# Turning a residual from features to tokens by DVE squares and DMAs in place of the tensor engine

## The chip, the core and the metric

One Trainium2 chip; the kernel runs on one of its cores. The metric is the device time of one execution in microseconds (us). The kernel before takes 696.79 us, the median of three runs (696.49 to 696.87).

Engines: PE (TensorE: matmuls, and transposes by a matmul with the identity), DVE (VectorE), ACT (ScalarE), POOL (GpSimd) and SP (SyncE, which issues most DMAs). Each works through its own queue in order; semaphores tie them together.

## The reference

One layer of a decoder on 512 tokens with 1024 features, in float32:

```python
h = rms_norm(x, mix_norm)
z = h @ w_in                       # u_A | v_A | c_q | c_kv | k_rope | gate_A | gate_B
y_a = chunked_spatial_gating(gelu(u_a), gelu(v_a), ...)   # 4 chunks of 128 tokens, 8 groups
y_b = latent_attention(c_q, c_kv, k_rope, ...)            # 8 heads, causal
x = x + (sigmoid(g_a) * y_a + sigmoid(g_b) * y_b) @ w_out
up = causal_depthwise_conv(rms_norm(x, ffn_norm) @ w_up)  # 2 x 2816 channels, width 3
gate, val = split(up)
x = x + (silu(gate) * val) @ w_down
out = rms_norm(x, final_norm)
```

The x after the mixers is the residual of this text. It is needed twice: by features, as the input of the up-projection, and by tokens, where the result of the down-projection is added to it.

## The kernel before

Tiles have 128 partitions. Matrices of float32 are split into a rounded part (H or h, made by ACT) and a rest (L or l, made by DVE), and each product is three matmuls (`mm3`, L79 to L82): H by H, H by L, L by H. A weight tile of 128x1024 is loaded by SP (`wtile`, names wr_...), and `wsplit` makes wh_... on ACT (L70) and wl_... on DVE (L71). Three buffers each serve raw tiles, wh and wl.

Stages: small projections and attention inputs, attention and gates by head, the output projection (`pout0` to `pout7`, L563 to L580), which leaves the residual by features in x1 (eight tiles x1[j] of 128 features by 512 tokens) and its normed halves in h0f to h7f; the up-projection; the down-projection.

The up-projection is a loop over n = 0 to 21 (L653). Each n makes two up groups, `up(2n)` and `up(2n+1)`, of 24 matmuls on PE into a bank `pup`, and a convolution on ACT and DVE for each (z is its scaled input, y its sum); `a_sides` builds from the results aT the left operands of the down-projection (a1h, a1l, s1, s4). In passes n = 4 to 11 `x1_turn` (L645) turns the residual from features to tokens: four transposes on PE (L649) into a bank pt and one ACT copy back into x1's own place (L650). In passes 12 to 17 `fill` (L604) names the load of the weight tiles r1_0, r1_2, ... r1_10 (R[0] to R[5]), which have memory of their own.

The down-projection is seven products, m1, m5, m6, m4, m3, m7, m2, each over the six weight tiles in R, in that order on PE. After R[g] is split, POOL adds the next weights onto it by an accumulating DMA, or SP loads it anew. `plus` and `done` (L726, L729) add products to the residual by tokens, `finish` (L736) norms and stores it.

A scheduler sets the order on each engine at build time: by the order of the source, by what its model of time holds ready, and by when a buffer's memory is free. A DMA of SP also waits for one of eight lanes (DMAHW0 to DMAHW7), so for an earlier DMA on the same lane.

Of the kernel before, what the change touches and what calls it, by code (L numbers as in the profile page):

```python
# [7 lines left out]
F32 = mybir.dt.float32  # L8
# [15 lines left out]
NF = DFF // P  # L24
# [18 lines left out]
def block_kernel(ctx, tc, xT, pos, w_s, w_v, w_g, w_q, w_kv, w_o, w_u, w_d,  # L43
                 ws_t, bs, vg, vb, par, cst, fnl, out):
    nc = tc.nc
    V, A, T, G, SY = nc.vector, nc.scalar, nc.tensor, nc.gpsimd, nc.sync
# [61 lines left out]
    ident = cstt[:, CI:CI + P]  # L108
# [66 lines left out]
    cqL = [mx.tile([P, S], F32R, name=f"cqL{i}") for i in range(2)]  # L175
    ckH = mx.tile([P, S], F32R, name="ckH")
    ckL = mx.tile([P, S], F32R, name="ckL")
    vA2 = [hp.tile([P, 2 * D], F32, tag=f"d{t}", name=f"vA{t}") for t in range(2)]
    vA = [vA2[t // 2][:, (t % 2) * D:(t % 2 + 1) * D] for t in range(NT)]

    with tc.tile_pool(name="st", bufs=2) as st:

# [22 lines left out]
        for j in range(KC):  # L205
# [7 lines left out]
            lo = half * S  # L213
# [3 lines left out]
            for f in range(4):  # L217
                c = slice(lo + f * P, lo + (f + 1) * P)
# [321 lines left out]
    with tc.tile_pool(name="mg", bufs=2) as mg:  # L540
        for h in range(H):
            zb = zbs[h] if h in zbs else gate("b", 2 * H + h)
            pm = bank(f"pm{h}")
            c = slice(h * P, (h + 1) * P)
            for n in range(NT):
                T.matmul(pm[:, n * P:(n + 1) * P], lhsT=vA[n][:, c], rhs=wst[:, h], start=True, stop=True)
            t2 = mg.tile([P, S], F32, tag="t2", name=f"t2{h}")
            V.tensor_tensor(out=t2.rearrange("p (n t) -> p n t", n=NT),
                            in0=pm.rearrange("p (n t) -> p n t", n=NT),
                            in1=bsb[:, h:h + 1].to_broadcast([P, NT, P]), op=ALU.add)  # L550
            V.tensor_tensor(out=t2, in0=uT[h], in1=t2, op=ALU.mult)
            zz = mg.tile([P, S], F32, tag="zz", name=f"zz{h}")
            V.tensor_tensor(out=zz, in0=zb, in1=yB[h], op=ALU.mult)
            V.tensor_tensor(out=zz, in0=zz, in1=t2, op=ALU.add)
            mH.append(uy.tile([P, S], F32R, tag=f"u{h}", name=f"mH{h}"))
            mL.append(uy.tile([P, S], F32R, tag=f"y{h}", name=f"mL{h}"))
            split(mH[h], mL[h], zz)


        x1t = [hp.tile([P, NT, NT, P], F32, tag=f"d{t}", name=f"x1_{t}") for t in range(2)]  # L560
        x1 = [x1t[j // NT][:, j % NT].rearrange("p t c -> p (t c)") for j in range(KC)]
        acc2 = hp.tile([P, S], F32, name="acc2")
        for j in range(KC):  # L563
            SY.dma_start(x1[j], xT[j])
            raw = wtile(w_o[j], f"o{j}")
            wh, wl = wsplit(raw, f"o{j}")
            po = bank(f"pout{j}")
            for h in range(H):
                c = slice(h * P, (h + 1) * P)
                mm3(po, wh[:, c], wl[:, c], mH[h], mL[h], h == 0, h == H - 1)  # L570
            V.tensor_tensor(out=x1[j], in0=po, in1=x1[j], op=ALU.add)
            htiles(j, "f")
            g_ = part[:, PFF + j:PFF + j + 1]
            A.mul(hH[j], x1[j], g_)
            V.scalar_tensor_tensor(out=hL[j], in0=x1[j], scalar=g_, in1=hH[j].bitcast(F32),
                                   op0=ALU.mult, op1=ALU.subtract)
# [18 lines left out]
    NS = len(steps)  # L595
    B11, B12, B21, B22 = (w_d[k, f] for k in range(2) for f in range(2))

    R = [fp.tile([P, (hi - lo) * S], F32, name=f"r1_{lo}") for lo, hi in steps]

    def cols(g):  # L600
        lo, hi = steps[g]
        return slice(lo * S, hi * S)

    def fill(q, g, add=True):  # L604
        if add:
            G.dma_start(R[g], q[:, cols(g)], accum_op=ALU.add)  # L606
        else:
            SY.dma_start(R[g], q[:, cols(g)])

# [32 lines left out]
                               op0=ALU.mult, op1=ALU.add)  # L642
        return y

    def x1_turn(t, hf):  # L645

        pt = bank(f"pt{t}{hf}")
        for q in range(NT):
            T.transpose(pt[:, q * P:(q + 1) * P], x1t[hf][:, q, t, :], ident)  # L649
        A.copy(x1t[hf][:, :, t, :], pt.rearrange("p (q c) -> p q c", q=NT))  # L650

    with tc.tile_pool(name="f2", bufs=2) as f2:
        for n in range(NF):  # L653
# [12 lines left out]
            if n % 4 == 3 or n == NF - 1:
                a_sides(n // 4 * 2, n // 2 + 1)
            if 4 <= n < 12:
                x1_turn((n - 4) // 2, n % 2)
            if 12 <= n < 12 + NS:  # L670
                fill(B11, n - 12, False)

# [43 lines left out]

    def res(t, f):

        return x1t[f][:, :, t, :]

    def b3(t):
        return t.rearrange("p (q c) -> p q c", q=NT)

    def plus(t, f, t_):  # L726
        V.tensor_tensor(out=res(t, f), in0=res(t, f), in1=b3(t_), op=ALU.add)

    def done(t, f, p_, op=ALU.add):  # L729
        V.tensor_tensor(out=res(t, f), in0=res(t, f), in1=b3(p_), op=op)  # L730
        j_ = dp.tile([P, S], F32, tag="j", name=f"j{t}{f}", bufs=2)
        A.activation(out=b3(j_), in_=res(t, f), func=AF.Square, accum_out=ms[:, t, f:f + 1])
        if f:
            V.tensor_tensor(out=res(t, f), in0=res(t, f), in1=b3(gfb[:, S:]), op=ALU.mult)

    def finish(t):  # L736

        V.tensor_scalar(out=ms[:, t, 2:3], in0=ms[:, t, 0:1], scalar1=ms[:, t, 1:2], scalar2=1.0 / D,
                        op0=ALU.add, op1=ALU.mult)
        V.tensor_scalar(out=ms[:, t, 2:3], in0=ms[:, t, 2:3], scalar1=EPS, scalar2=None, op0=ALU.add)  # L740
        G.tensor_tensor(out=ms[:, t, 3:4], in0=ms[:, t, 2:3], in1=mhalf[:, 0:1], op=ALU.pow)
        r_ = ms[:, t, 3:4]
        V.scalar_tensor_tensor(out=res(t, 0), in0=res(t, 0), scalar=r_, in1=b3(gfb[:, :S]),
                               op0=ALU.mult, op1=ALU.mult)
        A.mul(res(t, 1), res(t, 1), r_)
        SY.dma_start(out[t, :, :S], res(t, 0))
        A.dma_start(out[t, :, S:], res(t, 1))
# [143 lines left out]
```

## Time and profile before

| | |
|---|---|
| median of three runs | 696.79 us |
| the profiled execution | 697.01 us, its span 695.3 us |
| busy: PE, DVE, ACT, POOL | 684.6, 522.6, 353.9, 36.0 us |
| chain of waits | PE 96%, DVE 1%, issue 1% |
| mean granted clock of TensorE | 0.996 |
| DMA | 78.67 MB, mean 113 GB/s |

Busy times say how much each engine works; the chain says whose work decides the end. Here both name PE, which is almost never idle. The span runs from the first to the last instruction; the rest of an execution's time lies around it.

### The profile page before, as it was taken

What the parts mean: (1) busy time and instruction counts of PE and PEld (TensorE: products, weight loads), DVE (VectorE), ACT (ScalarE), POOL (GpSimd) and SP (SyncE); (2) the same over time, 40 slices, a digit from 0 to 9 for tenths busy, and PEclk for the clock granted to TensorE, in tenths of its full rate; (3) what the DMA queues carried; (4) which work ended last, traced back from release to release, by engine and by line L of the source; (5) the groups of instructions that cost most, each with busy time, mean ns of one, the idle gap of its engine ahead of it and who ended that gap; (6) DMA issues with size and microseconds to landing.
All of it is one profiled execution on the core that took longest, in us unless ns stands there. A gap on an engine that the chain in (4) does not pass through costs nothing.

```text
span 695.3 us, 8489 instructions
## 1 busy us (share of the span) xinstructions
PE 684.6 (98%) x3183; PEld 569.4 (82%) x3183; DVE 522.6 (75%) x859; ACT 353.9 (51%) x519; POOL 36.0 (5%) x42
## 2 busy tenths in 40 slices
PE   9999999999999999999999999999999999999994
PEld 6888888888888888888888888888888888888883
DVE  7966699877768678855577868778677789579884
ACT  6465556775765552343354344444344335565672
POOL 0000110000000000000100000000000002330201
PEclk9999999999999999999999999999999999999998
DMA  8424522131120112353542222223322236997824
GB/s 269 153 78 139 186 84 83 61 115 31 61 88 34 62 61 91 109 177 107 180 170 90 92 91 90 92 90 99 114 91 91 91 91 118 197 187 202 159 76 122
DMA packets 28026, 78.67 MB, mean 113 GB/s; under 512 B 3024, under 2 KB 7632, under 8 KB 27984
## 3 DMA queue, kind: packets, MB, share of 16 engines
q1 hardware_dynamic: 21408, 62.92, 27.4%
q0 software_dynamic: 3456, 11.54, 9.3%
q10 hardware_dynamic: 3120, 3.67, 1.7%
q8 instruction: 25, 0.41, 0.2%
q14 instruction: 17, 0.14, 0.1%
HBM read 76.02 MB, written 2.10 MB: 112 GB/s over the span
## 4 chain that ended last, share of the span: by engine, by line
PE 96%; DVE 1%; issue 1%; POOL 0%; ACT 0%; POOLq 0%
PE pup L80 12%; PE pup L82 12%; PE pup L81 11%; PE m L82 4%; PE m L81 4%; PE m L80 4%; PE pout L81 2%; PE pv L80 2%; PE pout L80 2%; PE pza L81 2%; PE pza L80 2%; PE pzb L80 2%; PE pzb L82 2%; PE pzu L81 2%; PE pzb L81 2%; PE pv L82 2%
## 5 line engine op out<-in xcount | busy, mean ns | idle before, releaser
L70 ACT CAST wh_u<-wr_u 128x1024 fp32r<-128x1024 f32 x44 | 46.3, 1051 | 84.4 <-issue 49.6
L71 DVE TENSOR_TENSOR wl_u<-wr_u,wh_u 128x1024 fp32r<-128x1024 f32 x44 | 53.9, 1224 | 9.9 <-ACT wh_u L70 9.6
L635 DVE TENSOR_TENSOR z<-pup,r 128x512 f32<-128x512 f32 x44 | 30.3, 690 | 40.3 <-PE pup L82 40.3
L82 PE MATMUL m<-wh_m,al_m 128*128 128x512 f32 x132 | 51.5, 390 | 0.6 <-DVE al_m L77 0.6
L80 PE MATMUL m<-wh_m,ah_m 128*128 128x512 f32 x132 | 51.4, 389 | 0.0
L81 PE MATMUL m<-wl_m,ah_m 128*128 128x512 f32 x132 | 51.4, 389 | 0.0
L70 ACT CAST wh_g<-wr_g 128x1024 fp32r<-128x1024 f32 x24 | 25.2, 1049 | 49.4 <-issue 30.6
L71 DVE TENSOR_TENSOR wl_m<-r,wh_m 128x1024 fp32r<-128x1024 f32 (+1 forms) x36 | 40.7, 1131 | 6.3 <-ACT wh_m L70 6.3
L70 ACT CAST wh_m<-r 128x1024 fp32r<-128x1024 f32 (+1 forms) x36 | 35.3, 980 | 19.6 <-PE m L82 19.1
L637 ACT ACTIVATE y<-z,part 128x512 f32<-128x512 f32 x44 | 35.7, 814 | 2.6 <-DVE z L635 2.4
L663 ACT ACTIVATE y<-y 128x512 f32<-128x512 f32 x22 | 13.9, 633 | 45.0 <-DVE y L641 45.0
L606 POOL DMA_DIRECT2D r<-in_w_d_dram x24 | 21.4, 890 | 287.0 <-DVE wl_m L71 270.7
L71 DVE TENSOR_TENSOR wl_g<-wr_g,wh_g 128x1024 fp32r<-128x1024 f32 x24 | 29.4, 1223 | 7.2 <-ACT wh_g L70 7.1
L641 DVE SCALAR_TENSOR_TENSOR y<-z,part,y 128x512 f32<-128x512 f32 x44 | 33.0, 751 | 1.4
L639 DVE SCALAR_TENSOR_TENSOR y<-z,part,y 128x512 f32<-128x512 f32 x44 | 32.8, 747 | 0.7 <-ACT y L637 0.7
L82 PEld LDWEIGHTS m<-wh_m,al_m 128*128 128x128 f32 x132 | 24.8, 188 | 6.1 <-DVE al_m L77 1.0
L81 PEld LDWEIGHTS m<-wl_m,ah_m 128*128 128x128 f32 x132 | 24.8, 188 | 5.2
L80 PEld LDWEIGHTS m<-wh_m,ah_m 128*128 128x128 f32 x132 | 24.8, 188 | 5.2
L81 PE MATMUL pout<-mL,wh_o 128*128 128x512 f32 x64 | 25.3, 395 | 0.0
L80 PE MATMUL pout<-mH,wh_o 128*128 128x512 f32 x64 | 25.0, 394 | 0.0
L82 PE MATMUL pout<-mH,wl_o 128*128 128x512 f32 x64 | 24.9, 389 | 0.0
L77 DVE TENSOR_TENSOR al_m<-aT,ah_m 128x1024 fp32r<-128x1024 f32 (+1 forms) x12 | 13.6, 1134 | 11.9 <-ACT ah_m L76 11.9
(565 smaller groups left out, 2004.0 us busy)
## 6 DMA issues: line engine op xcount, KB each, us to landing
wr_u<-in_w_u_dram SPq DMA_DIRECT2D x44, 512.0 KB, 3.3
wr_g<-in_w_g_dram SPq DMA_DIRECT2D x24, 512.0 KB, 3.4
r<-in_w_d_dram POOLq DMA_DIRECT2D x20, 512.0 KB, 7.2
r<-in_w_d_dram SPq DMA_DIRECT2D x10, 512.0 KB, 6.1
x<-in_xT_dram SPq DMA_DIRECT2D x16, 256.0 KB, 4.5
wr_v<-in_w_v_dram SPq DMA_DIRECT2D x8, 512.0 KB, 4.1
wr_o<-in_w_o_dram SPq DMA_DIRECT2D x8, 512.0 KB, 3.2
wr_m<-in_w_d_dram SPq DMA_DIRECT2D x5, 512.0 KB, 3.5
```

The source lines that it names most:

```text
L70: A.copy(th[:, lo:hi], raw[:, lo:hi])
L71: V.tensor_tensor(out=tl[:, lo:hi], in0=raw[:, lo:hi], in1=th[:, lo:hi].bitcast(F32), op=ALU.subtract)
L77: V.tensor_tensor(out=tl, in0=src, in1=th.bitcast(F32), op=ALU.subtract)
L80: T.matmul(o, lhsT=wh, rhs=xh, start=start, stop=False)
L81: T.matmul(o, lhsT=wh, rhs=xl, start=False, stop=False)
L82: T.matmul(o, lhsT=wl, rhs=xh, start=False, stop=stop)
L606: G.dma_start(R[g], q[:, cols(g)], accum_op=ALU.add)
L635: V.tensor_tensor(out=z[:, 2:], in0=pz, in1=r2, op=ALU.mult)
L637: A.activation(out=y, in_=z[:, 2:], func=AF.Identity, scale=part[:, w + 2:w + 3], bias=part[:, PCB + f:PCB + f + 1])
L639: V.scalar_tensor_tensor(out=y, in0=z[:, 1:S + 1], scalar=part[:, w + 1:w + 2], in1=y, op0=ALU.mult, op1=ALU.add)
L641: V.scalar_tensor_tensor(out=y, in0=z[:, 0:S], scalar=part[:, w:w + 1], in1=y, op0=ALU.mult, op1=ALU.add)
L663: A.activation(out=yg, in_=yg, func=AF.Silu)
```

## The change

x1 becomes one tile of memory "d" (and so does vA, which holds it earlier). DVE transposes each x1[j] in squares of 32 by 32 into a new tile xq (`squares`, two calls in each of the passes n = 0 to 3). 128 DMAs on SP then move the squares to their places in a tile xt, by tokens (`x1_turn`, eight DMAs of 32x4x32 elements in each of the passes n = 4 to 19). xt has the tag "d" too, so it takes x1's memory. xq0 to xq3 share the memory of r1_0 to r1_6, and `fill` is called in the last six passes, in the order 4, 5, 0, 1, 2, 3. The functions of the down-projection index xt by rows of 512 in place of pieces of 128.

```diff
--- before.py
+++ after.py
@@ -175,8 +175,8 @@
     cqL = [mx.tile([P, S], F32R, name=f"cqL{i}") for i in range(2)]
     ckH = mx.tile([P, S], F32R, name="ckH")
     ckL = mx.tile([P, S], F32R, name="ckL")
-    vA2 = [hp.tile([P, 2 * D], F32, tag=f"d{t}", name=f"vA{t}") for t in range(2)]
-    vA = [vA2[t // 2][:, (t % 2) * D:(t % 2 + 1) * D] for t in range(NT)]
+    vA4 = hp.tile([P, NT, D], F32, tag="d", name="vA")
+    vA = [vA4[:, t] for t in range(NT)]
 
     with tc.tile_pool(name="st", bufs=2) as st:
 
@@ -557,8 +557,8 @@
             split(mH[h], mL[h], zz)
 
 
-        x1t = [hp.tile([P, NT, NT, P], F32, tag=f"d{t}", name=f"x1_{t}") for t in range(2)]
-        x1 = [x1t[j // NT][:, j % NT].rearrange("p t c -> p (t c)") for j in range(KC)]
+        x1t = hp.tile([P, KC, S], F32, tag="d", name="x1")
+        x1 = [x1t[:, j] for j in range(KC)]
         acc2 = hp.tile([P, S], F32, name="acc2")
         for j in range(KC):
             SY.dma_start(x1[j], xT[j])
@@ -595,13 +595,17 @@
     NS = len(steps)
     B11, B12, B21, B22 = (w_d[k, f] for k in range(2) for f in range(2))
 
-    R = [fp.tile([P, (hi - lo) * S], F32, name=f"r1_{lo}") for lo, hi in steps]
+    xq = [fp.tile([P, D], F32, tag=f"r{q}", name=f"xq{q}") for q in range(KC // 2)]
+    R = [None] * NS
 
     def cols(g):
         lo, hi = steps[g]
         return slice(lo * S, hi * S)
 
     def fill(q, g, add=True):
+        if R[g] is None:
+            lo, hi = steps[g]
+            R[g] = fp.tile([P, (hi - lo) * S], F32, tag=f"r{g}", name=f"r1_{lo}")
         if add:
             G.dma_start(R[g], q[:, cols(g)], accum_op=ALU.add)
         else:
@@ -642,12 +646,20 @@
                                op0=ALU.mult, op1=ALU.add)
         return y
 
-    def x1_turn(t, hf):
-
-        pt = bank(f"pt{t}{hf}")
-        for q in range(NT):
-            T.transpose(pt[:, q * P:(q + 1) * P], x1t[hf][:, q, t, :], ident)
-        A.copy(x1t[hf][:, :, t, :], pt.rearrange("p (q c) -> p q c", q=NT))
+    def squares(j):
+        V.transpose(out=xq[j // 2][:, (j % 2) * S:(j % 2 + 1) * S], in_=x1[j])
+
+    xt = []
+
+    def x1_turn(j, rows):
+
+        if not xt:
+            xt.append(hp.tile([P, NT, D], F32, tag="d", name="xt"))
+        q = xq[j // 2][:, (j % 2) * S:(j % 2 + 1) * S].rearrange("p (t c f) -> p t c f", t=NT, c=NT)
+        for a in rows:
+            for c in range(NT):
+                SY.dma_start(xt[0][32 * c:32 * c + 32, :, j * P + 32 * a:j * P + 32 * a + 32],
+                             q[32 * a:32 * a + 32, :, c])
 
     with tc.tile_pool(name="f2", bufs=2) as f2:
         for n in range(NF):
@@ -665,10 +677,13 @@
             V.tensor_tensor(out=aT[:, i], in0=yg, in1=yv, op=ALU.mult)
             if n % 4 == 3 or n == NF - 1:
                 a_sides(n // 4 * 2, n // 2 + 1)
-            if 4 <= n < 12:
-                x1_turn((n - 4) // 2, n % 2)
-            if 12 <= n < 12 + NS:
-                fill(B11, n - 12, False)
+            if n < 4:
+                squares(2 * n)
+                squares(2 * n + 1)
+            elif n < 20:
+                x1_turn((n - 4) // 2, (0, 1) if n % 2 == 0 else (2, 3))
+            if n >= NF - NS:
+                fill(B11, (n - NF + NS + 4) % NS, False)
 
 
 
@@ -718,20 +733,17 @@
 
     def res(t, f):
 
-        return x1t[f][:, :, t, :]
-
-    def b3(t):
-        return t.rearrange("p (q c) -> p q c", q=NT)
+        return xt[0][:, t, f * S:(f + 1) * S]
 
     def plus(t, f, t_):
-        V.tensor_tensor(out=res(t, f), in0=res(t, f), in1=b3(t_), op=ALU.add)
+        V.tensor_tensor(out=res(t, f), in0=res(t, f), in1=t_, op=ALU.add)
 
...
```

The rest of the diff replaces `b3(...)` by its argument in `done` and `finish`.

DVE in the kernel before, at the end of the up-projection (z32 belongs to group 41, z43 to the last group, 43; wl_m10 is the split of r1_0 for the product m1):

```order
L635 TENSOR_TENSOR z32_4838<-pup41_4812,r2_3086 128x512
L71 TENSOR_TENSOR wl_m10_4942<-r1_0_3092,wh_m10_4941 128x1024
L639 SCALAR_TENSOR_TENSOR y32_4839<-z32_4838,part_67,y32_4839 128x512
...
L635 TENSOR_TENSOR z21_4877<-pup42_4852,r2_3086 128x512
...
L635 TENSOR_TENSOR z43_4916<-pup43_4890,r2_3086 128x512
L71 TENSOR_TENSOR wl_m12_4952<-r1_4_3094,wh_m12_4951 128x1024
L639 SCALAR_TENSOR_TENSOR y43_4917<-z43_4916,part_67,y43_4917 128x512
L641 SCALAR_TENSOR_TENSOR y43_4917<-z43_4916,part_67,y43_4917 128x512
```

DVE at the same place in the changed kernel:

```order
L645 SCALAR_TENSOR_TENSOR y32_4926<-z32_4925,part_67,y32_4926 128x512
L677 TENSOR_TENSOR aT_3085<-y10_4887,y32_4926 128x512
...
L639 TENSOR_TENSOR z43_5005<-pup43_4979,r2_3084 128x512
L650 STREAM_TRANSPOSE xq2_3092<-x1_2764 128x512 x2
L643 SCALAR_TENSOR_TENSOR y43_5006<-z43_5005,part_67,y43_5006 128x512
L645 SCALAR_TENSOR_TENSOR y43_5006<-z43_5005,part_67,y43_5006 128x512
...
L77 TENSOR_TENSOR al_m58_5092<-s1_3086,ah_m58_5091 128x768
L71 TENSOR_TENSOR wl_m10_5033<-r1_0_4759,wh_m10_5032 128x1024
L71 TENSOR_TENSOR wl_m11_5038<-r1_2_4853,wh_m11_5037 128x1024
```

The splits of r1_0 to r1_4 for m1 stood beside the last up groups and stand now behind all of the stage's work; the transposes of x1[4] and x1[5] into xq2 stand behind z43.

SP in the kernel before, early in the up-projection (wr_u6 is the weight tile of up group 6):

```order
L59 DMA wr_u5_3318<-in_w_u_dram 128x1024
L608 DMA r1_0_3092<-in_w_d_dram 128x1024
L608 DMA r1_2_3093<-in_w_d_dram 128x1024
L608 DMA r1_4_3094<-in_w_d_dram 128x1024
L59 DMA wr_u6_3358<-in_w_u_dram 128x1024
L608 DMA r1_6_3095<-in_w_d_dram 128x1024
L608 DMA r1_8_3096<-in_w_d_dram 128x1024
L59 DMA wr_u7_3396<-in_w_u_dram 128x1024
L608 DMA r1_10_3097<-in_w_d_dram 128x512
```

SP in the changed kernel, behind the last weight tiles of the up-projection (wr_m20 to wr_m22 are loads for the last product):

```order
L59 DMA wr_m20_5682<-in_w_d_dram 128x1024
L59 DMA wr_m21_5704<-in_w_d_dram 128x1024
L59 DMA wr_m22_5744<-in_w_d_dram 128x1024
L661 DMA xt_3524<-xq0_3090 32x4x32 x32
L661 DMA xt_3524<-xq1_3091 32x4x32 x32
L661 DMA xt_3524<-xq2_3092 32x4x32 x32
L661 DMA xt_3524<-xq3_3093 32x4x32 x24
L612 DMA r1_0_4759<-in_w_d_dram 128x1024
L661 DMA xt_3524<-xq3_3093 32x4x32 x8
L612 DMA r1_2_4853<-in_w_d_dram 128x1024
L612 DMA r1_4_4933<-in_w_d_dram 128x1024
L612 DMA r1_6_5019<-in_w_d_dram 128x1024
```

The loads of r1_0 to r1_6 moved from the start of the up-projection to behind 120 or all of the 128 DMAs that move squares, and these stand behind the last weight load.

The head of those DMAs on SP in the changed kernel, with the semaphores waited for (DVE for the transposes, DMAHW for the lanes):

```order
L661 DMA xt_3524<-xq0_3090 32x4x32 [waits DVE_49]
L661 DMA xt_3524<-xq0_3090 32x4x32 x4
L661 DMA xt_3524<-xq0_3090 32x4x32 [waits DMAHW5_49]
L661 DMA xt_3524<-xq0_3090 32x4x32 [waits DMAHW6_49]
L661 DMA xt_3524<-xq0_3090 32x4x32 [waits DMAHW7_49]
L661 DMA xt_3524<-xq0_3090 32x4x32 [waits DMAHW0_49]
L661 DMA xt_3524<-xq0_3090 32x4x32 [waits DMAHW1_49]
L661 DMA xt_3524<-xq0_3090 32x4x32 [waits DMAHW2_49]
```

From the sixth on each waits for a lane, and the lanes come round in eights.

DVE at the head of the up-projection, before (ms_f is the mean square for the norm of the residual):

```order
L580 TENSOR_TENSOR acc2_2767<-acc2_2767,sq2_7_3075 128x512
L146 TENSOR_SCALAR ms_f_3137<-pm_f_3132 128x4
L71 TENSOR_TENSOR wl_u3_3243<-wr_u3_3240,wh_u3_3242 128x1024
L134 SCALAR_TENSOR_TENSOR dL_f_3173<-cstt_69,rt_f_3138,dH_f_3172 128x128 x4
L71 TENSOR_TENSOR wl_u4_3283<-wr_u4_3280,wh_u4_3282 128x1024
```

and in the changed kernel:

```order
L580 TENSOR_TENSOR acc2_2765<-acc2_2765,sq2_7_3073 128x512
L650 STREAM_TRANSPOSE xq0_3090<-x1_2764 128x512 x2
L650 STREAM_TRANSPOSE xq1_3091<-x1_2764 128x512 x2
L146 TENSOR_SCALAR ms_f_3133<-pm_f_3128 128x4
L650 STREAM_TRANSPOSE xq3_3093<-x1_2764 128x512
L71 TENSOR_TENSOR wl_u3_3241<-wr_u3_3238,wh_u3_3240 128x1024
L134 SCALAR_TENSOR_TENSOR dL_f_3169<-cstt_69,rt_f_3134,dH_f_3168 128x128 x4
L650 STREAM_TRANSPOSE xq3_3093<-x1_2764 128x512
```

Six of the eight transposes stand here, four of them ahead of ms_f.

## Rows read from the trace of the kernel before

**Rows 1.** The page: busy time, the chain's shares by engine, one costly group.
```profile
PE 684.6 (98%) x3183; PEld 569.4 (82%) x3183; DVE 522.6 (75%) x859; ACT 353.9 (51%) x519; POOL 36.0 (5%) x42
...
PE 96%; DVE 1%; issue 1%; POOL 0%; ACT 0%; POOLq 0%
...
L70 ACT CAST wh_u<-wr_u 128x1024 fp32r<-128x1024 f32 x44 | 46.3, 1051 | 84.4 <-issue 49.6
```
**Rows 2.** Timeline of PE, heads of up groups: start, duration, instruction; the copies.
```profile
403.65 0.48 PE L80 MATMUL pup<-h0f,wh_u 128*128 128x512 f32 x1
...
415.00 0.48 PE L80 MATMUL pup<-h0f,wh_u 128*128 128x512 f32 x1
...
504.58 0.39 PE L80 MATMUL pup<-h0f,wh_u 128*128 128x512 f32 x1
...
515.47 0.39 PE L80 MATMUL pup<-h0f,wh_u 128*128 128x512 f32 x1
...
L650 ACT COPY x<-pt x8: 575/582/583, 392.9 to 472.4; 128x512 f32<-128x512 f32 x8
```
**Rows 3.** Timeline of PE where the up-projection ends.
```profile
580.52 0.39 PE L82 MATMUL pup<-h7f,wl_u 128*128 128x512 f32 x1
580.75 0.39 PE L80 MATMUL m<-wh_m,a1h 128*128 128x512 f32 x1
```
**Rows 4.** Timeline of ACT: casts of weights for m1 and m5.
```profile
569.90 1.04 ACT L70 CAST wh_m<-r 128x1024 fp32r<-128x1024 f32 x1
...
591.87 1.05 ACT L70 CAST wh_m<-r 128x1024 fp32r<-128x1024 f32 x1 [2.14 <-PE m L82]
```
**Rows 5.** Timeline of DVE; in brackets idle time before, and its releaser.
```profile
342.48 0.16 DVE L146 TENSOR_SCALAR ms_f<-pm_f 128x4 f32<-128x4 f32 x1 [2.88 <-PE pm_f L120]
...
563.53 0.69 DVE L616 TENSOR_TENSOR s<-aT 128x512 f32<-128x512 f32 x1
...
570.98 1.23 DVE L71 TENSOR_TENSOR wl_m<-r,wh_m 128x1024 fp32r<-128x1024 f32 x1 [0.22 <-ACT wh_m L70]
...
581.69 0.68 DVE L635 TENSOR_TENSOR z<-pup,r 128x512 f32<-128x512 f32 x1
```
**Rows 6.** Timeline of SP's queue: start of the first, time over all, count.
```profile
13.51 0.43 SPq L200 DMA_DIRECT2D part<-in_par_dram  x1
13.98 0.43 SPq L201 DMA_DIRECT2D post<-in_pos_dram  x1
14.46 0.43 SPq L202 DMA_DIRECT2D cstt<-in_cst_dram  x1
...
339.69 1.28 SPq L608 DMA_DIRECT2D r<-in_w_d_dram  x3
```
**Rows 7.** Waits of SP's queue: us in total, times, longest.
```profile
SPq L59 <- DVE wl_u L71: 223.7, 44, 6.4
```
**Rows 8.** DMA issues by line: count, KB each, median us to landing.
```profile
wr_u<-in_w_u_dram SPq DMA_DIRECT2D x44, 512.0 KB, 3.3
...
r<-in_w_d_dram POOLq DMA_DIRECT2D x20, 512.0 KB, 7.2
r<-in_w_d_dram SPq DMA_DIRECT2D x10, 512.0 KB, 6.1
x<-in_xT_dram SPq DMA_DIRECT2D x16, 256.0 KB, 4.5
...
out_dram<-x SPq DMA_DIRECT2D x4, 256.0 KB, 2.9
...
gb<-in_vg_dram ACTq DMA_DIRECT2D x2, 256.0 KB, 9.5
```
**Rows 9.** Windows: PE, PEld, DVE, ACT, POOL busy, granted clock, DMA share, GB/s.
```profile
690.30:694.00 3.70, 0.00 (x0) 0.00 (x0) 0.05 (x1) 0.01 (x1) 0.00 (x0) 0.50 0.53 144
```
**Rows 10.** Timeline of PE at the head of the kernel.
```profile
5.92 0.63 PE L81 MATMUL pS<-h0a,wh_s 128*128 128x512 f32 x1
6.35 0.63 PE L80 MATMUL pS<-h0a,wh_s 128*128 128x512 f32 x1
```

More of the change, by code (lines that the diff above doesn't have):

```diff
@@ L719, in res @@
     def res(t, f):
-        return x1t[f][:, :, t, :]
-    def b3(t):
-        return t.rearrange("p (q c) -> p q c", q=NT)
+        return xt[0][:, t, f * S:(f + 1) * S]
     def plus(t, f, t_):
-        V.tensor_tensor(out=res(t, f), in0=res(t, f), in1=b3(t_), op=ALU.add)
+        V.tensor_tensor(out=res(t, f), in0=res(t, f), in1=t_, op=ALU.add)
     def done(t, f, p_, op=ALU.add):
-        V.tensor_tensor(out=res(t, f), in0=res(t, f), in1=b3(p_), op=op)
+        V.tensor_tensor(out=res(t, f), in0=res(t, f), in1=p_, op=op)
         j_ = dp.tile([P, S], F32, tag="j", name=f"j{t}{f}", bufs=2)
-        A.activation(out=b3(j_), in_=res(t, f), func=AF.Square, accum_out=ms[:, t, f:f + 1])
+        A.activation(out=j_, in_=res(t, f), func=AF.Square, accum_out=ms[:, t, f:f + 1])
         if f:
-            V.tensor_tensor(out=res(t, f), in0=res(t, f), in1=b3(gfb[:, S:]), op=ALU.mult)
+            V.tensor_tensor(out=res(t, f), in0=res(t, f), in1=gfb[:, S:], op=ALU.mult)
     def finish(t):
@@ L742, in finish @@
         r_ = ms[:, t, 3:4]
-        V.scalar_tensor_tensor(out=res(t, 0), in0=res(t, 0), scalar=r_, in1=b3(gfb[:, :S]),
+        V.scalar_tensor_tensor(out=res(t, 0), in0=res(t, 0), scalar=r_, in1=gfb[:, :S],
                                op0=ALU.mult, op1=ALU.mult)
```

## The prediction

> **What bounds the kernel now.** I read the page first, from the top. The tensor engine (PE) is busy 98% of the span, and the chain of waits, followed back from the last instruction, lies on PE for 96% [rows 1]. So whatever is taken off PE shortens the run, and any hole in PE lengthens it by its full length. The other engines matter only through the question whether they deliver in time. Then I read the timeline of PE in the up-projection and at its end. The reader is to see there that PE passes from the last up group to the first matmul of m1, the first product of the down-projection, without a hole: 580.52 and 580.75, the usual step of 0.23 us [rows 3]. That works because the weights of m1 (the six tiles r) are loaded from 339.69 us on [rows 6], and ACT and DVE split the first of them at 569.90 and 570.98, ten microseconds ahead of need [rows 4, 5]. Last I read the queue of SP, which issues nearly all DMAs one after the other, for what one issue costs [rows 6].
>
> **What is removed.** 32 transposes on PE in eight groups of four, and eight ACT copies. A pass of two up groups takes 415.00 - 403.65 = 11.35 us with a group of transposes in it and 515.47 - 504.58 = 10.89 us without [rows 2]: 0.46 us a group, eight times, 3.7 us off PE. The ACT copies (8 x 0.58 us) go for nothing: ACT stood idle 84.4 us before the casts of this stage alone [rows 1, 2].
>
> **What is added.** Eight DVE transposes of 128x512, and 128 DMAs of 16 KB on SP. The source lists them through the whole up stage; the order of instructions as built says otherwise, and I go by the order. Six of the eight transposes (into xq0, xq1, xq3) stand at the start of the stage. The two into xq2 stand behind z43, the very last z of the stage, which needs the last up group. The turned tile xt takes the memory of x1, so no DMA may write it before all eight transposes have read x1. All 128 DMAs therefore stand on SP behind every weight load of the stage, and 120 of them ahead of the load of r1_0, the first weights of m1, since r1_0 to r1_6 now share memory with xq0 to xq3. In the kernel before those loads stood among wr_u5 to wr_u7.
>
> **The sum, step by step**, on the clock of the profiled execution.
> 1. The last up group ends at 580.52 + 0.39 = 580.91 us [rows 3]; 3.7 us earlier now: 577.2.
> 2. z43 takes 0.68 us [rows 5], then come the two transposes. No row shows one. Nearest is a DVE instruction of the same shape that reads and writes SBUF, 0.69 us; above it stands one of twice the elements, 1.23, far below it one of 4 columns, 0.16 [rows 5]. I take 0.69 twice: 577.2 + 0.68 + 1.38 = 579.3. The hand-over to SP is not counted.
> 3. 120 issues on SP. Three small loads (101.5, 2 and 144 KB), issued back to back, start at 13.51, 13.98 and 14.46: 0.47 and 0.48 us apart, with bytes that differ seventyfold. Three of 512 KB take 1.28 us together, 0.43 each [rows 6]. So an issue costs its time whatever it carries. I take 0.47, since by the order two of the three small loads, like these, also carry a wait for an earlier DMA: 120 x 0.47 = 56.4, and r1_0 is issued at 635.7.
> 4. r1_0 lands 3.3 us later, as the 512 KB of wr_u do when little else is under way; 6.1 is the row of r where six such loads compete with POOL's, and 2.9 the shortest row [rows 8]. ACT casts it in 1.05 [rows 4]. First matmul of m1 at 635.7 + 3.3 + 1.05 = 640.05, where it was 580.75: 59.3 us later. ACT and DVE run out of other work within some ten microseconds, and PE at once: m1 is first on PE's queue, and every other product stands behind it.
> 5. The start of m1. PE has idled for 63 us. The granted clock is 0.50 where PE idles at the end of the kernel before [rows 9], which is 1.2 GHz in place of 2.4. At the head of the kernel, after idling, large matmuls start 5.92 and 6.35 us into the span, 0.43 us apart [rows 10], where the step is 0.23 later on. The twelve matmuls of the first weight tile then take 12 x 0.43 = 5.2 us in place of 12 x 0.23 = 2.8, and the third of them, as now ordered, waits for DVE's 1.23 us of splitting behind 0.86 us of matmuls: 2.4 + 0.4 = 2.8 us. r1_2 is issued 9 places after r1_0, 4.2 us, and so comes in time behind that tile's 5.6 us.
> The Trainium skill (TensorE: Matmul & The Clock Gate, Part 1) says that the idle array sits at the lower clock and that sustained work releases it. The rows agree; if the array kept its clock through the hole, the sum would be 2.4 us less.
> 6. Behind m1 nothing new. POOL adds the next weights onto r1_0 after DVE's split; the add lands in 7.2 us [rows 8], so at about 640 + 1.2 + 7.2 = 648.4. The first cast of the next product came at 591.87 [rows 4], 11.1 us after m1's start, and comes now at about 654.
> Sum: 59.3 + 2.8 = 62.1 us. The profiled execution took 697.0 us, 1.7 beside its span of 695.3, and lies 0.2 above the median of the three runs, 696.8. So 697.0 + 62.1 = 759.1; I say 759.
>
> **What I cost at nothing, and its cover.** Six early transposes: four stand ahead of the mean square ms_f, for which DVE waited 2.88 us before 342.48 [rows 5]; 4 x 0.69 = 2.8 just fills that. At 1.23 each they would push the norm's chain, and PE's matmuls in it, by some 2.0 us. Rows of xt are contiguous where those of x1 were pieces of 128: the same shapes on DVE and ACT, hence 0; the last store lands in 2.9 us [rows 8], of which better rows may save some tenths. The loads of x wait for one tile more of the gating matmuls, some tenths too, and the sums that read them stand behind 24 output matmuls (24 x 0.23 = 5.5 us).
>
> The Trainium skill (DMA: Bandwidth & Descriptors, Rules for kernel authors) tells to coalesce many small transfers, since under 64 KB one pays mostly overhead; this change makes 128 of 16 KB. The rows say which overhead binds here, the issue. By the same page's fit, 2.0 us a DMA plus its bytes, eight under way would give an estimate of 0.26 us each, less than an issue takes, and the sum would stay as it is.
>
> **Rivals.**
> - The train is paced by landings, not by the issue. Each DMA waits for one that stands eight places ahead (the lanes 5, 6, 7, 0, 1 in turn, in the order with waits), so landing decides from 8 x 0.47 = 3.8 us up. For it: these DMAs move pieces of 128 bytes from SBUF to SBUF, which no row shows, and x lands in 4.5 us, gb in 9.5 [rows 8]. Against: stores from SBUF in pieces of 512 bytes land in 2.9. At 4.5 us: 120 x 0.56 = 67.5 in place of 56.4, so 770; at 9.5 it would be 845.
> - The DMAs go out under the up stage, as the source lists them, and only PE's 3.7 us are seen: 697.0 - 3.7 = 693.3, faster. It decides if the train, 60 us long, ends before the first weights of m1 are wanted at about 565, so if it begins before 505. For it: the source, and SP's idle time between the weight loads (223.7 us of waiting for DVE [rows 7]). Against: the order, in which the train waits for transposes behind z43.
> - The issue is cheaper for a DMA of 32 partitions. At 0.42, just under the shortest row [rows 6], 120 x 0.42 = 50.4: 753. This one I keep inside my forecast.
>
> **How the numbers follow.** The forecast, 759, has 0.83. Inside it: spacing 0.42 to 0.52 (-6 to +6), transposes 0.16 to 1.23 (-1.1 to +3.1 with the norm's delay), landing 2.9 to 6.1 (-0.4 to +2.8), m1's start 0 to 5 us (-2.8 to +2.2); not all fall to one side, so about 750 to 771. Paced by landings has 0.13, from 765 up, most of it around 770. Under the up stage has 0.03, and 0.01 goes to no change by a cover that I overlooked. Under 0.2% a difference cannot be told from none here. Faster 0.03, same 0.01, slower 0.96. Range 749 to 777: it takes in the nearer part of the landing-paced case.
>
> **What would show it.** On the page after, the 40 slices have a hole of three to four slices in PE from about 577 to 640 us, and PE's share falls from 98% to about 90%. The timeline of SP shows the first xt some 2 us behind the last up group and 128 issues about 0.47 us apart. The chain of waits passes through SP's queue for about 56 us. The granted clock falls to 0.50 in the hole, and matmuls start 0.43 us apart just behind it. No group pt is left on PE, the up stage is 3.7 us shorter, and m5 to m2 take what they took. The prediction is wrong if PE starts m1 directly behind the last up group, if issues lie 0.3 or 0.7 us apart, or if PE waits again between m1 and m5.

## The result, and the profile after

| | before | after |
|---|---|---|
| median | 696.83 us (4 runs, 696.49 to 697.94) | 783.07 us (4 runs, 782.53 to 784.55) |
| the profiled execution, its span | 697.01, 695.3 us | 783.48, 781.5 us |
| mean granted clock | 0.996 | 0.940 |

The changed kernel is slower by 12.4%: the ratio is 1.1239, 95% interval 1.1226 to 1.1253. The forecast was 759, the range 749 to 777. The hole was foreseen where it stands; it is 86.4 us long where 62.9 were foreseen (577.2 to 640.05).

The page of the changed kernel: busy times, two of the lines of 40 slices (19.5 us each; tenths busy, and the granted clock), the chain by engine, and a costly group with the idle time ahead of it.

```profile
PE 684.7 (88%) x3151; PEld 567.1 (73%) x3151; DVE 527.3 (67%) x867; ACT 350.7 (45%) x511; POOL 34.8 (4%) x42
...
PE   9999999999999999999999999999950000999995
...
PEclk9999999999999999999999999999985555899998
...
PE 77%; SPq 10%; DVE 7%; DMA 2%; issue 2%; ACT 0%; POOL 0%; POOLq 0%; DVEq 0%
...
L80 PE MATMUL m<-wh_m,a1h 128*128 128x512 f32 x22 | 9.8, 466 | 86.4 <-ACT wh_m L70 86.4
```

PE's 98% [rows 1] have become 88%, and the idle time that came in is one gap of 86.4 us ahead of m1. The chain, which lay on PE for 96%, now spends 10% on SP's queue.

The timeline of PE, at the start of the up stage, at its end and at the start of m1 (before: [rows 3]):

```profile
336.65 0.39 PE L80 MATMUL pup<-h0f,wh_u 128*128 128x512 f32 x1
...
577.26 0.39 PE L82 MATMUL pup<-h7f,wl_u 128*128 128x512 f32 x1
...
664.01 1.22 PE L80 MATMUL m<-wh_m,a1h 128*128 128x512 f32 x2 [86.36 <-ACT wh_m L70]
...
668.85 0.63 PE L81 MATMUL m<-wl_m,a1h 128*128 128x512 f32 x1
669.27 0.63 PE L82 MATMUL m<-wh_m,a1l 128*128 128x512 f32 x1
```

Three windows of it, the hole, the start of m1 and a stretch behind it (columns as in [rows 9]; the granted clock is the third number from the end):

```profile
577.70:664.00 86.30, 0.00 (x0) 0.00 (x0) 7.27 (x13) 2.93 (x4) 0.00 (x0) 0.52 0.21 36
664.00:670.00 6.00, 5.95 (x13) 3.94 (x14) 1.54 (x2) 1.04 (x1) 1.06 (x1) 0.50 0.70 218
672.00:674.00 2.00, 2.00 (x10) 1.67 (x9) 0.95 (x2) 1.48 (x2) 0.97 (x2) 1.00 1.10 211
```

PE ended the up stage in time, lay idle at the lower clock (1.2 GHz), and started m1 with matmuls 0.42 to 0.43 us apart.

The timeline of DVE behind the last up group, with z43 (L639) and the two late transposes (beside [rows 5]):

```profile
577.19 1.22 DVE L77 TENSOR_TENSOR al_m<-s,ah_m 128x1024 fp32r<-128x1024 f32 x1
578.33 0.69 DVE L639 TENSOR_TENSOR z<-pup,r 128x512 f32<-128x512 f32 x1
579.05 1.30 DVE L650 STREAM_TRANSPOSE xq<-x 128x512 f32<-128x512 f32 x2
```

The timeline of SP's queue in the gap (beside [rows 6]); a row gives the start of the first DMA, the time over all, and their count:

```profile
580.38 78.39 SPq L661 DMA_DIRECT2D xt<-xq  x120
658.82 0.59 SPq L612 DMA_DIRECT2D r<-in_w_d_dram  x1
659.45 5.09 SPq L661 DMA_DIRECT2D xt<-xq  x8
664.58 1.63 SPq L612 DMA_DIRECT2D r<-in_w_d_dram  x3
```

The DMA issues by line, KB each and median us to landing (beside [rows 8]):

```profile
xt<-xq SPq DMA_DIRECT2D x128, 16.0 KB, 1.8
...
out_dram<-xt ACTq DMA_DIRECT2D x4, 256.0 KB, 2.8
out_dram<-xt SPq DMA_DIRECT2D x4, 256.0 KB, 2.6
```

So 120 issues took 78.44 us (658.82 - 580.38), 0.654 each where the forecast had 0.47. They land in 1.8 us, so three are under way at a time, not the eight that the lanes allow. That speaks for the issue as what paces the train; experiments 4 and 6 test it.

### The profile page after: what moved, and what is told of

Its sections match the earlier page's. It is cut to its first block, busy times and chain, and to the rows that moved or that the text cites. A ratio compares the mean times of both kernels' runs of the same rounds, so it can differ in the third digit from the quotient of the medians.

```text
span 781.5 us, 8572 instructions
## 1 busy us (share of the span) xinstructions
PE 684.7 (88%) x3151; PEld 567.1 (73%) x3151; DVE 527.3 (67%) x867; ACT 350.7 (45%) x511; POOL 34.8 (4%) x42
## 4 chain that ended last, share of the span: by engine, by line
PE 77%; SPq 10%; DVE 7%; DMA 2%; issue 2%; ACT 0%; POOL 0%; POOLq 0%; DVEq 0%
PE pup L82 10%; PE pup L80 10%; PE pup L81 10%; SPq L661 10%; PE m L82 4%; PE m L81 4%; PE m L80 4%; PE pout L81 2%; PE pout L80 2%; PE pzb L80 2%; PE pzb L82 2%; PE pzb L81 2%; PE pout L82 2%; PE pv L80 2%; PE pv L82 2%
## 5 line engine op out<-in xcount | busy, mean ns | idle before, releaser
L80 PE MATMUL m<-wh_m,a1h 128*128 128x512 f32 x22 | 9.8, 466 | 86.4 <-ACT wh_m L70 86.4
L80 PEld LDWEIGHTS m<-wh_m,a1h 128*128 128x128 f32 x22 | 4.7, 223 | 88.1 <-ACT wh_m L70 87.3
L639 DVE TENSOR_TENSOR z<-pup,r 128x512 f32<-128x512 f32 x44 | 30.3, 690 | 38.1 <-PE pup L82 38.1
L675 ACT ACTIVATE y<-y 128x512 f32<-128x512 f32 x22 | 13.9, 633 | 46.0 <-DVE y L645 45.9
```

What stands on the lines that cost most here:

```text
L80: T.matmul(o, lhsT=wh, rhs=xh, start=start, stop=False)
L639: V.tensor_tensor(out=z[:, 2:], in0=pz, in1=r2, op=ALU.mult)
```

## The experiments

Two questions were open. Why do the two transposes of xq2 stand behind z43, when nothing that they compute needs the last up group? And what makes one issue cost 0.65?

### 1. A name of its own for the memory

In the change `xq[q]` has the tag `r{q}`, so xq2 has the tag "r2". The norm factor `r2 = fp.tile([P, S], F32, name="r2")` has no tag, so its name is its tag, and the pool gives both the same memory. z43 is the last reader of the norm factor. The order shows where the transposes stand, and the prediction took that from it without asking why.

```diff
-    xq = [fp.tile([P, D], F32, tag=f"r{q}", name=f"xq{q}") for q in range(KC // 2)]
+    xq = [fp.tile([P, D], F32, tag=f"x{q}", name=f"xq{q}") for q in range(KC // 2)]
...
-            R[g] = fp.tile([P, (hi - lo) * S], F32, tag=f"r{g}", name=f"r1_{lo}")
+            R[g] = fp.tile([P, (hi - lo) * S], F32, tag=f"x{g}", name=f"r1_{lo}")
```

> The four tiles xq and the six tiles R get names of their own for their memory (x0 to x5 in place of r0 to r5); nothing else is edited. Theory (shared name): the norm factor r2 has no tag, so its own name is its tag, and xq2 and R[2], tagged r2 too, wait for r2's last reader, the last z of the up stage; that alone put two transposes, and with them all 128 DMAs, behind the stage. Then the renamed kernel has eight early transposes, its 128 issues of 0.64 us (82 us) lie in SP's idle time of the up stage (223.7 us of waiting in the kernel before), the hole of 86.4 us before m1 is gone, and the time is 696.8 - 3.3 (the transposes taken off PE) = about 693.5, between 692.5 and 695. Rival (the train costs wherever it stands): SP is late with weight loads by up to 6 x 0.64 us a group, PE waits in the up stage, and the time is above 697, up to 696.8 + 82 x (share not hidden).

Measured: 692.14 us (5 runs, 691.99 to 693.51) beside 696.6 before; ratio 0.9934, interval 0.9922 to 0.9947. The shared name was the whole loss, and without it the change is a gain of 4.5 us. That is 0.4 below the expected range: the expectation counted PE's transposes alone, and the end of the kernel is shorter too, 8.1 us from the last matmul in place of 9.15 (step 5 below). SP's queue at the start of the up stage of this kernel:

```profile
344.01 0.33 SPq L59 DMA_DIRECT2D wr_u<-in_w_u_dram  x1
346.98 3.33 SPq L661 DMA_DIRECT2D xt<-xq  x5
350.40 0.53 SPq L59 DMA_DIRECT2D wr_u<-in_w_u_dram  x1
350.98 6.39 SPq L661 DMA_DIRECT2D xt<-xq  x10
```

The 128 issues are the same, dear ones too, but they lie between the weight loads. SP's wait for DVE's split of wr_u is the cover that they use up: it fell from 223.7 us [rows 7] to 124.2, and PE lost nothing.

```profile
SPq L59 <- DVE wl_u L71: 124.2, 25, 5.6
```

PE at the seam of the up stage and m1 in this kernel:

```profile
576.26 0.39 PE L82 MATMUL pup<-h7f,wl_u 128*128 128x512 f32 x1
576.49 0.39 PE L80 MATMUL m<-wh_m,a1h 128*128 128x512 f32 x1
```

### 2. The renamed kernel without the turning

```diff
-            if n < 4:
-                squares(2 * n)
-                squares(2 * n + 1)
-            elif n < 20:
-                x1_turn((n - 4) // 2, (0, 1) if n % 2 == 0 else (2, 3))
...
-        return xt[0][:, t, f * S:(f + 1) * S]
+        return x1t[:, 2 * t + f]
```

> The renamed kernel without the turning: no transposes of DVE, no xt DMAs; the residual is added as it lies, in features, so this part of the output is left out. It shows what is left to gain once the turning costs nothing. Theory: the DVE transposes and the train are hidden in the renamed kernel, so both take the same, about 693.5, within 0.5 us. Rival: the train or the transposes still cost PE something under the up stage; then this one is faster than the renamed kernel by that amount, 1 to 4 us.

Measured: 692.20 us (5 runs, 691.61 to 692.96), ratio 0.9934, interval 0.992 to 0.9947: the same as with the turning. Eight transposes on DVE and 128 DMAs cost nothing that can be measured where they are covered.

### 3. Only xq2 shares, then only r1_4 shares

Two tiles had the tag "r2" beside the norm factor: xq2, and R[2] (r1_4). From the renamed kernel, one of them was given the tag back in each run (the first edit in one, the second in the other).

```diff
-    xq = [fp.tile([P, D], F32, tag=f"x{q}", name=f"xq{q}") for q in range(KC // 2)]
+    xq = [fp.tile([P, D], F32, tag="r2" if q == 2 else f"x{q}", name=f"xq{q}") for q in range(KC // 2)]
...
-            R[g] = fp.tile([P, (hi - lo) * S], F32, tag=f"x{g}", name=f"r1_{lo}")
+            R[g] = fp.tile([P, (hi - lo) * S], F32, tag="r2" if g == 2 else f"x{g}", name=f"r1_{lo}")
```

> The renamed kernel, but xq2 alone is tagged r2 again, so it shares memory with the norm factor r2 as in the change; the six tiles R keep names of their own. Theory (xq2's sharing alone is the cause): two transposes stand behind the last z, the whole train behind them, m1 starts at about 664, time 783 within 1 us. Rival (R[2], which shared the name too, or the sharing between xq and R held the train): the train goes out under the up stage, m1 starts at about 577, and the time is 692 to 695.

Measured: 781.86 us (one run). xq2's sharing alone brings the whole hole back; PE at the start of m1:

```profile
662.45 1.22 PE L80 MATMUL m<-wh_m,a1h 128*128 128x512 f32 x2 [85.98 <-ACT wh_m L70]
```

> The renamed kernel, but R[2] (the tile r1_4, third weights of m1) alone is tagged r2 again; xq2 has a name of its own. Its load must then wait for the last z, at about 578 us, lands 3.5 to 4 us later and is cast in 1.05: ready at 582.5 to 583.2. A tile of weights feeds 12 matmuls of 0.227 us, so m1 wants the third one 5.4 us after its start at 576.5, at 581.9. Theory: m1 waits there once for 0.6 to 1.3 us, time 692.1 + 1 = 693. Rival (the load is covered, as POOL's adds and the earlier tiles give room): 692.1, no wait in PE's list.

Measured: 693.99 us (5 runs, 693.64 to 695.02), ratio 0.9966, interval 0.9953 to 0.9979; 1.85 us above the renamed kernel. PE at the third weight tile of m1:

```profile
582.81 0.73 PE L80 MATMUL m<-wh_m,a1h 128*128 128x512 f32 x2 [0.85 <-ACT wh_m L70]
584.15 0.50 PE L81 MATMUL m<-wl_m,a1h 128*128 128x512 f32 x1 [0.61 <-DVE wl_m L71]
```

The theory held in place, with 1.46 us of waiting a little more than it allowed. This second sharing was hidden in the changed kernel behind the first.

### 4. The train dealt out to two queues

```diff
-                SY.dma_start(xt[0][32 * c:32 * c + 32, :, j * P + 32 * a:j * P + 32 * a + 32],
+                (SY, A)[c % 2].dma_start(xt[0][32 * c:32 * c + 32, :, j * P + 32 * a:j * P + 32 * a + 32],
```

> The changed kernel as it was (late train), the 128 DMAs dealt out alternately to SP's and ACT's queues. Theory (the issue on one queue sets the pace): each queue keeps 0.64 us from issue to issue, r1_0 is issued at 580.4 + 60 x 0.644 = 619, m1 starts at about 624 in place of 664, time about 743. Rival (what paces is behind the queues: the DMA engines, the writing of 128-byte pieces, or the landing): each queue's issues lie 1.29 us apart, m1 starts at about 664, and the time stays 783.

Measured: 744.93 us (one run). The timelines of SP's queue, ACT's queue and PE:

```profile
580.00 39.42 SPq L661 DMA_DIRECT2D xt<-xq  x60
619.60 0.46 SPq L612 DMA_DIRECT2D r<-in_w_d_dram  x1
...
580.01 42.38 ACTq L661 DMA_DIRECT2D xt<-xq  x64
...
624.98 1.22 PE L80 MATMUL m<-wh_m,a1h 128*128 128x512 f32 x2 [47.71 <-ACT wh_m L70]
```

60 issues took 39.6 us on SP (619.60 - 580.00), 0.66 each, while ACT's queue issued 64 more at the same pace (42.38 us). The price is each queue's own; what is behind the queues isn't the limit at this rate.

### 5. What makes an issue dear

Two runs of the changed kernel with other shapes in the train. SBUF is the memory on the core in which the tiles lie; DRAM holds the kernel's inputs and outputs. The diff is cut from that of the first run; in it x is the part of xt that belongs to j, q and fl are xq as in the change and flat, and o is xT[j], in DRAM, cut as q is.

```diff
+                if j == 0:
+                    SY.dma_start(x[rc, :, f], q[ra, :, c])
+                elif j == 1:
+                    SY.dma_start(x[rc, a], fl[ra, c * P:(c + 1) * P])
+                elif j == 2:
+                    SY.dma_start(x[:, c, f], q[:, c, a])
...
+                elif j == 5:
+                    SY.dma_start(x[rc, :, f], o[ra, :, c])
```

> The changed kernel as it was (late train), but the eight groups of 16 DMAs have eight shapes, each on its own line (what is moved is not the turned residual in six of them). Measured is the spacing of issues in each group: j0 32 partitions x 4 x 32 from SBUF as in the change; j1 32 partitions x 128 contiguous on both sides (32 pieces of 512 B, the same bytes); j2 128 partitions x 32 (128 pieces of 128 B, two dimensions); j3 32 x 2 x 32 (64 pieces); j4 64 x 4 x 32 (256 pieces); j5 32 x 4 x 32 from DRAM; j6 source contiguous, destination in pieces of 32; j7 source in pieces, destination contiguous. Theory A (the shape's third dimension costs the issue): j1 and j2 0.47, all others 0.64, j3 and j4 too. Theory B (the number of 128-byte pieces sets the issue): 0.47 for j1, 0.5 to 0.55 for j3, 0.64 for j0 and j2, about 1.0 for j4. Theory C (reading from SBUF): j5 alone 0.47. Theory D (32 partitions): j2 alone 0.47, j4 in between.

Its timeline of SP: L667 is j0, L669 j1, L671 j2, L677 j4, L679 j5, L681 j6, L683 j7.

```profile
579.61 10.40 SPq L667 DMA_DIRECT2D xt<-xq  x16
590.05 10.09 SPq L669 DMA_DIRECT2D xt<-xq  x16
600.19 10.24 SPq L671 DMA_DIRECT2D xt<-xq  x16
...
631.08 5.31 SPq L677 DMA_DIRECT2D xt<-xq  x8
636.43 10.24 SPq L679 DMA_DIRECT2D xt<-in_xT_dram  x16
646.71 10.95 SPq L681 DMA_DIRECT2D xt<-xq  x16
```

All groups, the two left out too, cost 0.63 to 0.69 an issue: 32 pieces or 256, two dimensions or three, 32 partitions or 128. All four theories fell: no shape brought the price down, nor did a source in DRAM at the shape of the change. Left was the source at plain shapes, which a second run varied.

> The changed kernel as it was, with the 128 DMAs replaced by eight groups of 16 of other shapes, each on its own line; the turned residual is left out. Measured is what one issue takes. From DRAM to SBUF: j0 128 x 32 (pieces of 128 B), j1 32 x 128 (32 pieces of 512 B), j2 128 x 128, j6 128 x 512. From SBUF to SBUF: j3 128 x 128, j4 128 x 8 (pieces of 32 B), j5 128 x 512. From SBUF to DRAM: j7 128 x 128. Theory A (an SBUF source makes the issue dear; one of three dimensions does too): j0, j1, j2, j6 0.43, and j3, j4, j5, j7 0.59. Theory B (the pieces of the destination: anything that is cut out of a longer row of the tile, under its full length): j0 to j4 0.59, only j5 and j6 0.43 where lanes are free. Theory C (what is in the queue ahead: short landings, so that completions come in while the next is issued): the dear ones are those that land within 2 us, whatever their source, and 256 KB ones, landing later, cost 0.43.

Its timeline of SP: L681 is j7 (SBUF to DRAM), L667 j0 and L669 j1 (DRAM to SBUF), L675 j4 (SBUF to SBUF).

```profile
346.03 3.69 SPq L681 DMA_DIRECT2D out_dram<-xq  x8
...
579.62 7.79 SPq L667 DMA_DIRECT2D xt<-in_xT_dram  x16
587.46 7.38 SPq L669 DMA_DIRECT2D xt<-in_xT_dram  x16
...
614.72 8.33 SPq L675 DMA_DIRECT2D xt<-xq  x13
```

128x32 from DRAM costs 0.49 an issue (7.84 us from the first of 16 to the next group's first) where the same shape from SBUF cost 0.64 (j2 above); 32x128 costs 0.46 against 0.63; into DRAM from SBUF 0.47. So theory A is half right: a DMA from SBUF to SBUF is dear whatever its shape, even with pieces of 32 B. A source in SBUF alone is not, since j7 is cheap; that part of A fell. Theory B fell with j0 and j1, which are cut out of longer rows and cheap, and theory C with the same two, which land in 1.7 us. The groups of 256 KB (j5 0.71 an issue, j6 0.82) do not tell the price of the issue: the DMA engines were busy for 0.90 and 0.92 of the time there, against 0.14 in j1 and j4, so the transfers themselves may have set the pace. The three-dimensional 32x4x32 from DRAM was dear as well (0.64, j5 above), so there are two ways to the same price, and they don't add up: 32x4x32 from SBUF to SBUF costs no more than either. Why, these runs do not show.

### 6. The train at the price that the prediction used

```diff
-                SY.dma_start(xt[0][32 * c:32 * c + 32, :, j * P + 32 * a:j * P + 32 * a + 32],
-                             q[32 * a:32 * a + 32, :, c])
+                d, f = xt[0][:, c, j * P + 32 * a:j * P + 32 * a + 32], slice(32 * a, 32 * a + 32)
+                SY.dma_start(d, xT[j, :, f] if c < 3 else q[:, c, a])
```

> The changed kernel as it was (late train, 128 DMAs of 16 KB on SP), but three of each four DMAs read 128 x 32 from DRAM in place of the turned residual in SBUF, and the fourth moves 128 x 32 from SBUF, so that r1_0 still waits for the train; the residual is left out of the output by that. Theory (the price of one issue is what the prediction missed): 90 issues ahead of r1_0 now cost 0.475 and 30 cost 0.644, 62.1 us in place of 78.4; m1 starts at about 648 in place of 664, and the time falls from 783.1 by 16 to 767 (766 to 769). Rival (something else paces the train, the landings or the lanes' semaphores): the train stays near 78 us and the time at 783.

Measured: 766.41 us (4 runs, 766.06 to 768.04), ratio 1.1004, interval 1.0987 to 1.102. The start and the end of its train:

```profile
579.19 1.28 SPq L662 DMA_DIRECT2D xt<-in_xT_dram  x3
...
640.35 1.54 SPq L662 DMA_DIRECT2D xt<-in_xT_dram  x3
641.93 0.47 SPq L662 DMA_DIRECT2D xt<-xq  x1
642.45 0.59 SPq L612 DMA_DIRECT2D r<-in_w_d_dram  x1
```

From 579.19 to 642.45 are 63.3 us for 120 issues; m1 started at 647.53. Count, bytes and lanes are those of the change, so it was the price of the issue that the prediction missed. The first three issues, all from DRAM, took 1.28 us; three that stand behind an SBUF source took 1.54, so a dear DMA holds up the issue behind it.

### 7. PE kept busy in the hole

```diff
+    warm = bank("warm")
+    last = a1h[:, KH - 2:].rearrange("p k t -> p (k t)")
+    for _ in range(375):                               # 390 in the second run
+        T.matmul(warm, lhsT=last[:, S2:S2 + P], rhs=last, start=True, stop=True)
```

> The changed kernel with 375 matmuls of 128 x 512 on PE between the last up group and m1, whose result nobody reads; they keep PE busy for about 85 of the 86 us of the hole. Theory (the low clock costs m1's start, as the prediction's step 5 has it): the first matmuls of m1 start 0.23 us apart in place of 0.43, and the time falls by 2.4 to 3 us, to about 780. Rival (m1's second weight tile, issued after r1_0 and eight more DMAs, paces the start): with the clock kept the first twelve matmuls are done in 2.7 us, PE then waits 2 to 3 us for the second tile, and the time stays at 783 within 0.6.

Measured: 785.15 us (4 runs, 784.25 to 785.33), ratio 1.1269, interval 1.125 to 1.1288. The added matmuls ended 3.9 us ahead of m1, and m1's own started 0.43 us apart again until 669.40. So the run did not show m1 at the full clock; the second one, with more matmuls, does.

> As the run with 375 matmuls in the hole, but 390 of them, so that PE is busy until within about a microsecond of m1's start and the granted clock should still be 1.0 there. Theory (the second weight tile paces m1's start, not the clock): the first twelve matmuls start 0.23 us apart, PE then waits 2 to 3 us for the second tile, cast at about 671, and the time from m1's start to the end is 117.5 us as in the changed kernel, within 0.6. Rival (the clock costs m1's start 2.4 us or more): that time is 115 us or less.

Measured: 786.85 us (4 runs, 785.13 to 787.30), ratio 1.1295, interval 1.1276 to 1.1314. PE's timeline:

```profile
654.77 10.36 PE L693 MATMUL warm<-a1h 128*128 128x512 f32 x45
665.27 0.49 PE L80 MATMUL m<-wh_m,a1h 128*128 128x512 f32 x1
666.53 0.50 PE L81 MATMUL m<-wl_m,a1h 128*128 128x512 f32 x1 [0.77 <-DVE wl_m L71]
...
671.06 0.50 PE L80 MATMUL m<-wh_m,a1h 128*128 128x512 f32 x1 [1.74 <-ACT wh_m L70]
```

And two of the windows that were shown of the changed kernel:

```profile
577.70:664.00 86.30, 86.30 (x382) 71.48 (x381) 6.36 (x11) 1.65 (x2) 0.00 (x0) 1.00 0.21 36
664.00:670.00 6.00, 4.41 (x17) 2.77 (x16) 1.23 (x1) 1.09 (x2) 1.06 (x1) 1.00 0.54 161
```

The granted clock was 1.00 through the hole and behind it, the first tile's matmuls started 0.23 us apart, and what they won PE lost again waiting for the second tile. From m1's start to the end of the span are 783.1 - 665.27 = 117.8 us, in the changed kernel 781.5 - 664.01 = 117.5. That is one execution of each, for this run its fastest of four. The low clock cost m1 nothing that can be seen: the second weight tile, behind r1_0 and eight more dear issues, came no earlier after m1's start (ACT cast it from 669.97 here, 4.70 us behind that start, and 4.59 in the changed kernel). Both runs are 2 to 4 us slower than the changed kernel, part of it because their 120 issues took 80.5 to 80.9 us in place of 78.4; why, wasn't pursued.

## Why the prediction was wrong, step by step

Forecast and measured positions in the profiled execution; the last column is what each step adds to the miss.

| step | forecast | measured | adds |
|---|---|---|---|
| 1, last up group ends | 577.2 | 577.65 | +0.45 |
| 2, first issue of the train | 579.3 | 580.38 | +0.63 |
| 3, r1_0 issued | 635.7 | 658.82 | +22.04 |
| 4, m1 starts | 640.05 | 664.01 | +0.84 |
| 5 and 6, from there to the end of the span | 114.55 + 2.8 = 117.35 | 117.49 | +0.14 |
| around the span | 1.7 | 1.98 | +0.28 |
| sum | 759.1 | 783.48 | +24.4 |

**Step 1 was right.** The up stage went from 336.65 to 577.26, 240.61 us, where it had gone from 336.05 to 580.52, 244.47 us: 3.86 less, forecast 3.7. The 0.45 is a start of the stage that was 0.6 us later in this execution; in the renamed kernel the stage takes 240.62 and starts at 335.64.

**Step 2 was right in kind.** A transpose of 128x512 takes 0.69 us, as taken. z43 itself was late by about 0.7: DVE was still splitting a left operand (al_m, to 578.4) when the bank was ready, which the sum had left out.

**Step 3 failed: "an issue costs its time whatever it carries. I take 0.47".** The rows under it [rows 6] were loads from DRAM in plain rows, and among those the statement is true: bytes and pieces hardly matter, and neither did they among the shapes of the train (256 pieces cost 0.67, 32 pieces 0.63). But the rows held no DMA from SBUF to SBUF, and none of three dimensions; each of the two alone costs 0.64 here, and the train was both. Measured was 0.654 an issue, 78.44 us where the sum had 56.4. Experiment 6 put the cheap kind in three quarters of the train and got 15.2 of the 22 us back (63.3 in place of 78.44; the time fell by 16.7). The prediction gave 0.47 a spread of 0.42 to 0.52, as if this price were measured, when it was carried over from another kind of transfer. Rows that pointed to the dear side were there, though none shows 0.65: a store of the kernel before, out of SBUF in 512 pieces of 512 B, takes 0.47 on ACT and 0.38 on SP with no other issue ahead of it (0.37 and 0.33 in the changed kernel, where its rows are whole), a weight load that stands alone 0.33 on SP, and POOL's loads of r take 0.89. The cheap side, 0.42, rested on a loose reading: 0.43 each for three loads is their time over all divided by three, while the second and third of them started 0.48 apart.

**Step 4** was off by 0.84: r1_0 landed in 4.1 us, not 3.3 (issued at 658.82, cast from 662.91), with the last eight DMAs of the train issued behind it in that time.

**Step 5 came out right for a wrong reason.** m1 to m2, from the first matmul of m1 to the last of m2, took 109.36 us where they had taken 105.40: 3.96 more, nearly all of it in m1, forecast 2.8. The clock was as forecast, 0.52 in the hole and 0.50 up to 670; the rule that the prediction weighed there, of the lower clock of an idle array (the Trainium skill, TensorE: Matmul & The Clock Gate, Part 1), agrees with the trace. But in experiment 7 the clock decided nothing. The sentence that failed is "r1_2 ... comes in time behind that tile's 5.6 us": at the dear price r1_2 was issued 5.76 us after r1_0 (664.58), and DVE began its split at 669.68, so the tile came just when the slow matmuls were done:

```profile
668.60 1.04 ACT L70 CAST wh_m<-r 128x1024 fp32r<-128x1024 f32 x1 [4.64 <-DMA r<-in_w_d_dram]
...
669.68 1.23 DVE L71 TENSOR_TENSOR wl_m<-r,wh_m 128x1024 fp32r<-128x1024 f32 x1 [4.46 <-ACT wh_m L70]
...
669.70 1.14 PE L80 MATMUL m<-wh_m,a1h 128*128 128x512 f32 x2
```

Against that stands a gain of 1.0 us at the end of the kernel: from the last matmul to the end of the span 8.13 us in place of 9.15. The stores of contiguous rows land in 2.6 us on SP and 2.8 on ACT, where it was 2.9 [rows 8] and 3.3; the longest on ACT, 3.8 before, is 2.9 now. The forecast had "some tenths" for it and cost it at nothing.

**The rivals.** "Paced by landings" fell: landings of 1.8 us pace nothing at 0.65 an issue. Its time, 770, was nearer than the forecast's, by chance. "A cheaper issue" had the wrong sign. "Out under the up stage, 693.3" did not happen in the changed kernel, and is what the renamed one does: 692.1, with the train begun at 347 us, as its condition asked (before 505). What stood between the two was one tag, and the forecast of 0.03 for it was fair only for the code as built.

The rule that the prediction weighed, to coalesce small transfers (the Trainium skill, DMA: Bandwidth & Descriptors, Rules for kernel authors), points the right way: a DMA of 64x4x32 carries twice the bytes for nearly the same issue, 0.67 (experiment 5, j4).

## What to carry to other kernels

When an instruction stands later in the order than its data would have it, find the memory that it waits for before working out what the wait costs: here one tile's name was another's tag, and that turned a gain of 0.6% into a loss of 12%. Take the price of a transfer from a row of the same kind, the same in source, destination and dimensions; where no row has it, leave the range open to the dear side and multiply by the count before deciding how wide that is. A train of small DMAs is free where its queue idles between other loads, and costs its whole length as soon as a load that PE waits for stands behind it.

## What the runs showed of the hardware

- The issue of a DMA on SP's queue, back to back: DRAM to SBUF in plain rows 0.46 to 0.49 us, SBUF to DRAM 0.47, SBUF to SBUF 0.63 to 0.69 in every shape tried of 4 KB to 64 KB, and 32x4x32 from DRAM 0.64 (experiments 4 to 6).
- That price is per queue: SP and ACT issue at 0.66 side by side (experiment 4).
- SBUF to SBUF, 16 KB lands in 1.8 us in pieces of 128 B.
- The granted clock stays at 1.00 (2.4 GHz) through 390 matmuls whose result is not used, and m1 behind them runs at that clock. In the run with 375, after 3.9 us in which PE was idle, m1's matmuls started 0.43 us apart from 666.67 to 669.40, and the clock was 0.72 in the mean from 664 to 670.
